# TensorE in order of emission through the attention and the retention, and 18 filling steps ahead of the first scores

## The chip, the core and the metric

The kernel runs on one core of a Trainium2 chip. A core has five engines with an instruction queue each: TensorE (PE, matrix products; its weight loads are shown as PEld), VectorE (DVE), ScalarE (ACT), GpSimd (POOL) and SyncE (SP, which here only starts DMAs). Each engine works through its queue in order; where an instruction needs a result of another engine, it waits, and all that stands behind it in the same queue waits with it. The metric is the device time of one execution in microseconds (us); less is better.

## The reference

One layer of an encoder trunk, for 1024 tokens of 1024 features in float32:

```python
h = _swiglu(_rms_norm(x, ffn1_pre_norm[l]), ffn1_w_in[l], ffn1_w_out[l])
x = x + 0.5 * _rms_norm(h, ffn1_post_norm[l])
m = _token_mixing(_rms_norm(x, mix_pre_norm[l]), w_mix_in[l], ret_decay_fwd[l], ret_decay_bwd[l],
                  na_rel_bias[l], w_ret_out[l], w_na_out[l], w_mix_out[l], pos)
x = x + _rms_norm(m, mix_post_norm[l])
h = _swiglu(_rms_norm(x, ffn2_pre_norm[l]), ffn2_w_in[l], ffn2_w_out[l])
x = x + 0.5 * _rms_norm(h, ffn2_post_norm[l])
```

The middle part, `_token_mixing`, projects the tokens once with a wide matrix, and uses the pieces for two kinds of mixing:

```python
y = _bidirectional_retention(q, k, heads(rv, RET_V_DIM), decay_fwd, decay_bwd)   # 4 heads, chunks of 128 tokens
y_ret = (jax.nn.silu(rg) * y) @ w_ret_out
y_na = _neighborhood_attention(na_heads(nq), na_heads(nk), na_heads(nv), rel_bias) @ w_na_out  # 8 heads of 64
merged = jax.nn.sigmoid(g_ret) * y_ret + jax.nn.sigmoid(g_na) * y_na
return merged @ w_out
```

The neighbourhood attention lays the tokens on a grid of 16 rows and 64 columns; each query sees a window of 8 rows and 16 columns, with a learned bias per head, and takes a softmax over it.

## The kernel before

Every product is made of three products of split operands (`mm3`, lines 85 to 89): a float32 tile x is split by ACT into a rounded high part (`split`, line 60) and by DVE into the rest (line 61), and TensorE adds high by high, low by high and high by low. So each operand that TensorE reads costs one ACT and one DVE instruction first.

The program runs through these stages: the first feed-forward block, the projections for the mixing, the neighbourhood attention, the retention, the output projections, the second feed-forward block. The change touches the attention and the retention.

**The attention** (`na_cores`, line 688) works on 32 units: 4 pairs of heads by 8 units of 128 queries each. It is written as a pipeline over units:

- `scores` of unit i: for each of the two heads of the pair, two matmuls of 128x384 (line 744: high and low part of the query), then on DVE the bias and the maximum (745) and the negated maximum (747), on ACT the exponential (749), on DVE the reciprocal of the sum and the scaling (751, 753).
- `flip` of unit i-1: six transposes on TensorE (763) into two PSUM banks `pt`, then the split into `pth` (ACT) and `ptl` (DVE).
- `values` of unit i-2: nine matmuls of 128x256 (`mm3` with `vh`, `vl`), then two ACT copies into `ot` (779).

Between these parts stand calls of a **filler**. `fill(n)` takes n steps from the generator `products()`; a step is one `mm3`, three matmuls of 128x512 of the value projection of the retention (operands `wh`, `wl` with `a11h` and the like, 128 steps), then of the gates (384 steps in all), which nothing in the attention waits for. `NA_FILL` gives the numbers: 12 steps ahead of the first scores, then 2 after `scores` and 2 after `values` in each of 34 iterations. Filling steps of the projections bring their own loads and splits of weights (`wraw`, `wh`, `wl`).

At a change of the pair of heads the keys (`kraw`), the queries (`qraw`) and, for each group of columns, the values (`vraw`) are loaded by SP and split by ACT, DVE and POOL; the bias tiles `bt` are loaded by SP for nearly every unit.

**The retention** (`ret_cores`, line 872) works through 4 heads of 8 chunks: a backward pass that builds states (`update`), then per chunk a score product, the state update, the two products with the states (`cross`), the product `inner`, a norm, and two transposes two chunks later (`store`, 966). Filling steps stand between these too (`RET_FILL`): 14 ahead of the first transposes of the keys (`kdec`, 914), 2 to 4 at each place after that, and 2 ahead of each of the last three `store`. What the filler still holds after that is drained.

**What sets the order.** The order in which the Python code emits instructions isn't the order in the queues. Emission gives priorities; a scheduler then simulates the program with durations of its own, and puts next on each engine the instruction of the highest priority that is ready in its simulation. So an instruction that the simulation shows as waiting is passed by later ones that are ready: filling steps, scores of later units, or values. The queues are fixed then; the chip keeps to them whatever the real durations are.

Of the kernel before, what the change touches and what calls it, by code (L numbers as in the profile page):

```python
# [1 line left out]

# [1 line left out]

# [22 lines left out]
RH = 4  # L27
NHP = 4

NA_FILL = (12, 2, 2)  # L30
RET_FILL = (14, 2, 2, 4, 2, 3, 0, 1, 2)
FLIP_FILL = (8, 8, 8, 8, 2)
NA_UNITS = ((0, 0, 0), (3, 1, 0), (1, 0, 1), (1, 0, 2), (4, 1, 1), (4, 1, 2), (2, 0, 3), (5, 1, 3))
# [4 lines left out]
class Core:  # L38
# [97 lines left out]
    def out_proj(self, nk, lhs, wload, done, groups=((0, 1, 2), (3, 4, 5), (6, 7)), tail=3, lag=8, space=3):  # L136

        left = []  # L140

        def one(t, k, a, w):
            for e in [e for e in left if e[0] <= 0]:
                left.remove(e)
                f = e[1]()
                if f is not None:
                    left.append([2, f])
            for b in range(2):
                self.mm3(banks[t][b], a[t], w[b], k == 0, k == nk - 1)
            for e in left:  # L150
                e[0] -= 1

        for toks in groups:
            banks = {t: [self.bank() for _ in range(2)] for t in toks}
            tl = tail if len(toks) > 1 else 0
            for k in range(nk - tl):
                w, a = wload(k), lhs(k, toks)
                for t in toks:
                    one(t, k, a, w)
            last = [(k, lhs(k, toks), wload(k)) for k in range(nk - tl, nk)]  # L160
            for t in toks:
                for k, a, w in last:
                    one(t, k, a, w)
                f = done(t, banks[t])
                if f is not None:
                    left.append([max(lag, max([e[0] for e in left], default=-space) + space), f])
        return [f for _, f in left]


class Filler:  # L170
# [267 lines left out]
class LeftFactors:  # L438


    order = [j + h * FT // 2 for j in range(FT // 2) for h in range(2)]
# [588 lines left out]
def trunk_layer(ctx: ExitStack, tc, x, g1a, w1i, w1o, g1b, gma, wmt, wnv, wrv, logits, dtab, rope, bias,  # L1030
# [7 lines left out]
    c = Core(tc, const, wpool, psum, dram)  # L1038
# [219 lines left out]

    fill = Filler(products())
    dec = []  # L1260
    with tc.tile_pool(name="na", bufs=1) as na:
        na_cores(c, na, d, bias, fill, *NA_FILL, {24: lambda: dec.append(Decays(c, mix, logits, dtab))})
    dec = dec[0]
    fill.until("rv")
    with tc.tile_pool(name="ret", bufs=1) as ret:
        ret_cores(c, ret, mix, d, dec, fill, RET_FILL)
    y_stack = ExitStack()
    ypool = pool(y_stack, "y")
# [152 lines left out]
```

## Time and profile before

| | |
|---|---|
| median of 3 runs | 2334.3 us (2330.53 to 2337.57) |
| profiled execution | 2332.5 us, its span 2330.7 us |
| first feed-forward block and projections | 0 to about 998 us |
| attention (first filling step to last values) | 998 to 1232 us |
| retention | about 1232 to 1471 us |
| output projections and second feed-forward block | 1471 to 2331 us |
| PE idle outside 1000 to 1480 us | some 70 us, at the start, the end, and the borders of the feed-forward blocks |

Times in the profile are counted from the start of the span. "Busy" is the time in which an engine works on an instruction; matmuls overlap, so the start of one to the start of the next is the price of a matmul, not its duration. PEclk is the clock granted to TensorE as a share of full speed.

### The profile page before, as it was taken

Reading aid. Unit: us, or ns where it says so; the run is one execution under the profiler, and the core shown is the slowest. Engines: PE = TensorE matmul, PEld = TensorE weight load, DVE = VectorE, ACT = ScalarE, POOL = GpSimd, SP = SyncE. Lnnn points to the kernel's source line nnn. Section 1 sums busy time; section 2 is a strip of 40 time slices with the busy share of each in tenths; the row PEclk is TensorE's granted clock in tenths of the full one; section 3 lists DMA queues with packets and bytes.
Section 4 is the critical chain, followed back from the end, with each engine's and each line's share of the span. In section 5 each row is a group of like instructions: output and inputs, shape, how many; then the busy total and the mean of one; then the engine's idle time right before and its main releaser. Section 6 shows DMA issues by size and latency. Waiting matters only on the chain.

```text
span 2330.7 us, 30323 instructions
## 1 busy us (share of the span) xinstructions
PE 2226.6 (96%) x10288; PEld 1849.4 (79%) x10288; DVE 1677.0 (72%) x2939; ACT 1008.0 (43%) x2104; POOL 598.9 (26%) x749
## 2 busy tenths in 40 slices
PE   6999999999998999989889999998889999999998
PEld 5888888778886888877768888887668888887886
DVE  7887777745878588867865678545887778775575
ACT  6332222344553223367765676324633222234453
POOL 3144343300440144311101222101322434431032
PEclk9999999999998999999989999999999999999999
DMA  5355555576753444466634467765524555547674
GB/s 190 109 181 174 197 177 185 199 233 189 257 175 112 168 131 131 137 217 202 195 107 152 161 222 231 263 230 188 194 91 142 197 176 200 181 154 235 190 243 142
DMA packets 161884, 422.64 MB, mean 181 GB/s; under 512 B 19712, under 2 KB 47488, under 8 KB 161664
## 3 DMA queue, kind: packets, MB, share of 16 engines
q1 hardware_dynamic: 121248, 286.97, 38.4%
q0 software_dynamic: 40480, 133.72, 15.6%
q8 instruction: 81, 1.33, 0.2%
q14 instruction: 75, 0.61, 0.1%
HBM read 301.60 MB, written 123.21 MB: 182 GB/s over the span
## 4 chain that ended last, share of the span: by engine, by line
PE 84%; issue 6%; DVE 4%; DMA 2%; ACT 2%; POOL 1%; SPq 0%; POOLq 0%; DVEq 0%; ACTq 0%
PE ps L87 26%; PE ps L88 26%; PE ps L89 26%; PE pt L88 1%; PE pt L89 1%; PE pt L87 1%; DMA graw<-g0a 1%; PE pt L126 1%; DVE tmp L117 0%; DVE wl L61 0%; DMA graw<-m 0%; PE pt L914 0%; DMA kraw<-nk 0%; PE pt L966 0%; DVE gl L61 0%
## 5 line engine op out<-in xcount | busy, mean ns | idle before, releaser
L61 DVE TENSOR_TENSOR wl<-wraw,wh 128x512 fp32r<-128x512 f32 x662 | 460.3, 719 | 97.4 <-ACT wh L60 94.5
L60 ACT CAST wh<-wraw 128x512 fp32r<-128x512 f32 x670 | 391.7, 619 | 277.3 <-PE ps L88 110.0
L87 PE MATMUL ps<-wh,gh 128*128 128x512 f32 x612 | 239.2, 393 | 17.2 <-ACT gh L60 12.8
L88 PE MATMUL ps<-wl,gh 128*128 128x512 f32 x612 | 239.4, 391 | 0.0
L61 DVE TENSOR_TENSOR gl<-graw,gh 128x512 fp32r<-128x512 f32 (+2 forms) x178 | 128.9, 728 | 149.2 <-ACT gh L60 146.0
L89 PE MATMUL ps<-wh,gl 128*128 128x512 f32 x612 | 229.1, 392 | 1.1 <-DVE gl L61 1.1
L60 ACT CAST gh<-graw 128x512 fp32r<-128x512 f32 (+2 forms) x178 | 106.5, 602 | 210.6 <-PE ps L88 72.0
L87 PEld LDWEIGHTS ps<-wh,gh 128*128 128x128 f32 x612 | 115.5, 189 | 44.8 <-ACT gh L60 12.9
L526 POOL TENSOR_TENSOR q<-q,gain 128x512 f32<-128x512 f32 x30 | 58.1, 1958 | 334.4 <-PE ps L88 122.1
L89 PEld LDWEIGHTS ps<-wh,gl 128*128 128x128 f32 x612 | 114.8, 188 | 26.3 <-DVE gl L61 2.8
L88 PEld LDWEIGHTS ps<-wl,gh 128*128 128x128 f32 x612 | 115.5, 189 | 23.7
L60 ACT CAST wh<-t 128x512 fp32r<-128x512 f32 x58 | 36.1, 623 | 192.7 <-DVE t L384 192.6
L87 PE MATMUL ps<-a11h,wh 128*128 128x512 f32 x280 | 113.1, 404 | 1.9 <-DVE tmp L226 1.9
L89 PE MATMUL ps<-a11h,wl 128*128 128x512 f32 x280 | 111.7, 399 | 0.0
L88 PE MATMUL ps<-a11l,wh 128*128 128x512 f32 x280 | 111.4, 398 | 0.0
L87 PE MATMUL ps<-a12h,wh 128*128 128x512 f32 x280 | 110.6, 395 | 0.1
L88 PE MATMUL ps<-a12l,wh 128*128 128x512 f32 x280 | 109.8, 392 | 0.0
L89 PE MATMUL ps<-a12h,wl 128*128 128x512 f32 x280 | 109.6, 391 | 0.0
L87 PE MATMUL ps<-a22h,wh 128*128 128x512 f32 x280 | 109.5, 391 | 0.0
L89 PE MATMUL ps<-a22h,wl 128*128 128x512 f32 x280 | 109.2, 390 | 0.0
L88 PE MATMUL ps<-a22l,wh 128*128 128x512 f32 x280 | 109.1, 389 | 0.0
L400 DVE TENSOR_TENSOR c<-ps,gt 128x512 f32<-128x512 f32 x44 | 30.4, 691 | 107.2 <-PE ps L89 107.1
(362 smaller groups left out, 6006.6 us busy)
## 6 DMA issues: line engine op xcount, KB each, us to landing
wraw<-in_dram SPq DMA_DIRECT2D x243, 512.0 KB, 4.3
lead<-in_dram POOLq DMA_DIRECT2D x44, 256.0 KB, 3.9
g0s<-cmb POOLq DMA_DIRECT2D x44, 256.0 KB, 3.2
graw<-g0s SPq DMA_DIRECT2D x44, 256.0 KB, 2.8
wq<-in_dram POOLq DMA_DIRECT2D x44, 256.0 KB, 3.8
g1s<-cmb POOLq DMA_DIRECT2D x44, 256.0 KB, 2.7
graw<-g1s SPq DMA_DIRECT2D x44, 256.0 KB, 2.7
bt<-in_dram SPq DMA_DIRECT2D x24, 384.0 KB, 3.9
```

Source lines behind the costliest of these rows:

```text
L60: nc.scalar.copy(h, src)
L61: (eng or nc.vector).tensor_tensor(l, src, hf, ALU.subtract)
L87: mm(ps, a[0], b[0], start=start, stop=False, skip_group_check=more)
L88: mm(ps, a[0], b[1], start=False, stop=False, skip_group_check=more)
L89: mm(ps, a[1], b[0], start=False, stop=stop, skip_group_check=more)
L126: self.nc.tensor.transpose(pt[:, j * P:(j + 1) * P], h[:, j * P:(j + 1) * P], self.ident)
L400: self.last = self.read = tt(c21, p7, c12, ALU.add).ins
L526: (eng or c.nc.gpsimd).tensor_tensor(h if out is None else out, h, self.post[:, b * 512:(b + 1) * 512], ALU.mult)
```

## The change

```diff
-from contextlib import ExitStack
+from contextlib import ExitStack, contextmanager
...
-NA_FILL = (12, 2, 2)
+NA_FILL = (18, 2, 2)
...
+@contextmanager
+def in_order(c, engine):
+
+    traced = c.nc.cur_bb.bb.instructions
+    n = len(traced)
+    yield
+    prev = None
+    for i in c.nc.cur_bb.bb.instructions[n:]:
+        if i.engine == engine:
+            if prev is not None:
+                c.tc.add_manual_dep(i, prev.name, mybir.DependencyInfo(
+                    mybir.DependencyClass.NoSync, mybir.DependencyReason.DATA), reason="order")
+            prev = i
...
-    with tc.tile_pool(name="na", bufs=1) as na:
+    with tc.tile_pool(name="na", bufs=1) as na, in_order(c, mybir.EngineType.PE):
         na_cores(c, na, d, bias, fill, *NA_FILL, {24: lambda: dec.append(Decays(c, mix, logits, dtab))})
     dec = dec[0]
     fill.until("rv")
-    with tc.tile_pool(name="ret", bufs=1) as ret:
+    with tc.tile_pool(name="ret", bufs=1) as ret, in_order(c, mybir.EngineType.PE):
         ret_cores(c, ret, mix, d, dec, fill, RET_FILL)
```

`in_order` gives each PE instruction that is emitted inside the block a dependency on the PE instruction emitted before it. The dependency is of a kind that adds no semaphore and no wait: it only tells the scheduler that the one comes after the other. So inside the attention, and again inside the retention, TensorE's queue stands in the order of the code, filling steps included. The first instruction of a block has no such tie, and the other engines have none; their queues come from the same simulation, which now runs with another TensorE. The second edit puts 18 filling steps ahead of the first scores in place of 12; the six steps are missing at the end, since the filler holds the same 384 steps (and a mark behind the value projection that a call counts as one). Before, all calls together ask for 384 of these 385; now they ask for 390, and the last ones come up empty.

On each engine the kernel has the same instructions as before, but for two ACT_TABLE_LOAD on ACT that fall away. All queues are the same up to the first scores. From there to the output projection of the mixing they differ; behind that they are the same again.

The first place is TensorE's queue from the end of the second unit's scores to the fourth's, with the first transposes (`s` into `pt`) and the first of the nine value matmuls (`pth`, `vh`); the numbers tell buffers apart. Before:

```order
L744 MATMUL ps_8742<-k1_8603,ql_8623 128x384
L744 MATMUL ps_8807<-k0_8602,qh_8704 128x384
L744 MATMUL ps_8807<-k0_8602,ql_8705 128x384
L744 MATMUL ps_8811<-k1_8603,qh_8708 128x384
L744 MATMUL ps_8811<-k1_8603,ql_8709 128x384
L763 MATMUL pt_8775<-ident_69,s_8687 128x128 x3
L763 MATMUL pt_8781<-ident_69,s_8687 128x128 x3
L87 MATMUL ps_8843<-pth_8773,vh_8768 128x256
L744 MATMUL ps_8863<-k0_8602,qh_8753 128x384
L744 MATMUL ps_8863<-k0_8602,ql_8754 128x384
L744 MATMUL ps_8867<-k1_8603,qh_8757 128x384
L744 MATMUL ps_8867<-k1_8603,ql_8758 128x384
```

In the changed kernel, from the second unit's scores to the same transposes (lines are 15 higher behind `in_order`, so scores are L759 and transposes L778):

```order
L759 MATMUL ps_8766<-k0_8602,qh_8618 128x384
L759 MATMUL ps_8766<-k0_8602,ql_8619 128x384
L759 MATMUL ps_8770<-k1_8603,qh_8622 128x384
L759 MATMUL ps_8770<-k1_8603,ql_8623 128x384
L87 MATMUL ps_8627<-wh_8746,a12h_5400 128x512
L88 MATMUL ps_8627<-wl_8747,a12h_5400 128x512
L89 MATMUL ps_8627<-wh_8746,a12l_5401 128x512
L87 MATMUL ps_8628<-wh_8746,a12h_5400 128x512
L88 MATMUL ps_8628<-wl_8747,a12h_5400 128x512
L89 MATMUL ps_8628<-wh_8746,a12l_5401 128x512
L778 MATMUL pt_8803<-ident_69,s_8715 128x128 x3
L778 MATMUL pt_8809<-ident_69,s_8715 128x128 x3
```

Before, the scores of three units stand ahead of the first transposes, and no filling step between them and the transposes; now there are the scores of two, with two filling steps behind the second. The count of filling matmuls ahead of these transposes is 72 in both.

The second place is TensorE's queue four units later. Before:

```order
L744 MATMUL ps_9102<-k0_8602,qh_8975 128x384
L744 MATMUL ps_9102<-k0_8602,ql_8976 128x384
L744 MATMUL ps_9106<-k1_8603,qh_8979 128x384
L744 MATMUL ps_9106<-k1_8603,ql_8980 128x384
L87 MATMUL ps_9147<-pth_9066,vh_8907 128x256
L744 MATMUL ps_9169<-k0_8602,qh_8975 128x384
L744 MATMUL ps_9169<-k0_8602,ql_8976 128x384
L744 MATMUL ps_9173<-k1_8603,qh_8979 128x384
L744 MATMUL ps_9173<-k1_8603,ql_8980 128x384
L763 MATMUL pt_9135<-ident_69,s_9037 128x128 x3
L88 MATMUL ps_9147<-ptl_9067,vh_8907 128x256
L89 MATMUL ps_9147<-pth_9066,vl_8908 128x256
```

In the changed kernel, at about the same unit, from the last value matmul to the next filling step:

```order
L89 MATMUL ps_9175<-pth_9094,vl_8936 128x256
L87 MATMUL ps_8826<-wh_9147,a22h_6071 128x512
L88 MATMUL ps_8826<-wl_9148,a22h_6071 128x512
L89 MATMUL ps_8826<-wh_9147,a22l_6072 128x512
L87 MATMUL ps_8824<-wh_9151,a12h_5400 128x512
L88 MATMUL ps_8824<-wl_9152,a12h_5400 128x512
L89 MATMUL ps_8824<-wh_9151,a12l_5401 128x512
L759 MATMUL ps_9197<-k0_8602,qh_9003 128x384
L759 MATMUL ps_9197<-k0_8602,ql_9004 128x384
L759 MATMUL ps_9201<-k1_8603,qh_9007 128x384
L759 MATMUL ps_9201<-k1_8603,ql_9008 128x384
L87 MATMUL ps_8825<-wh_9151,a22h_6071 128x512
```

Before, the value matmuls of one unit are taken apart, and scores, transposes and values follow each other with no filling step between; the steps stand in long rows elsewhere. Now every unit has its six transposes and nine value matmuls together, and two filling steps stand on each side of the scores.

At the end of the retention the last `store` calls lose steps: after the last product with a state there stood some seven filling steps, two of them between the last two pairs of transposes; now two stand there, and the last two pairs follow each other.

## The prediction

> **What bounds the kernel.** I read the page's first part, then the stages by a table of windows, then TensorE's waits in the stages that the change touches.
>
> ```profile
> PE 2226.6 (96%) x10288; PEld 1849.4 (79%) x10288; DVE 1677.0 (72%) x2939; ACT 1008.0 (43%) x2104; POOL 598.9 (26%) x749
> core 0: us, PE busy (x) PEld busy (x) DVE busy (x) ACT busy (x) POOL busy (x), PEclk, DMA share, GB/s
> 1007.00:1232.00 225.00, 196.14 (x1042) 167.51 (x1041) 159.59 (x467) 155.26 (x393) 19.73 (x26) 0.93 0.55 172
> 1246.00:1472.00 226.00, 224.61 (x1290) 195.82 (x1289) 164.67 (x428) 140.90 (x365) 54.57 (x86) 1.00 0.59 191
> ```
>
> TensorE is the bound of the whole (96% busy), so the change can gain only where TensorE stands still or runs slowly. The attention (1007 to 1232) is such a place: 28.9 us idle, at a mean clock of 0.93. The retention (1246 to 1472) isn't: 1.4 us idle at full clock. The waits of the attention by who ended them:
>
> ```profile
> PE ps L87 <- ACT pth L60: 15.5, 11, 3.6
> PE pt L763 <- DVE s L753: 4.8, 2, 4.4
> PE ps L88 <- DVE ptl L61: 4.8, 4, 2.5
> PE ps L744 <- DVE nast L745: 2.0, 2, 1.0
> PE pt L763 <- DVE ptl L61: 1.6, 3, 0.7
> ```
>
> They add up to 28.7 us, 20.3 of them value matmuls that wait for their transposed weights (`pth`, `ptl`). The clock costs as well. One such wait, and the stretches in which the clock was half (the first of six, and the sum):
>
> ```profile
> 1202.63 0.54 PE L87 MATMUL ps<-pth,vh 128*128 128x256 f32 x1 [2.81 <-ACT pth L60]
> 1202.97 0.52 PE L744 MATMUL ps<-k,qh 128*128 128x384 f32 x1
> 1203.29 0.52 PE L744 MATMUL ps<-k,ql 128*128 128x384 f32 x1
> ...
> 1021.80:1028.60 6.80, 4.52 (x14) 3.76 (x15) 5.80 (x19) 5.57 (x16) 0.54 (x1) 0.50 0.88 337
> ...
> sum 30.60, PE 25.98 PEld 21.69 DVE 21.53 ACT 17.72 POOL 0.54; mean PE 4.33 PEld 3.62 DVE 3.59 ACT 2.95 POOL 0.09
> ```
>
> After the 2.81 us wait a score matmul takes 0.32 us from start to start (1202.97 to 1203.29). TensorE was busy for 25.98 us at half clock, so 13.0 us would do at full clock. Waits and clock together: 28.7 + 13.0 = 41.7 us that the attention could lose at most by this count.
>
> **The attention, part by part.** No work is added; what counts is how it is spread. The prices at full clock, from start to start:
>
> ```profile
> 1044.80 0.82 PE L763 MATMUL pt<-ident,s 128*128 128x128 f32 x6
> 1045.37 0.36 PE L87 MATMUL ps<-pth,vh 128*128 128x256 f32 x1
> ...
> 1046.52 0.34 PE L744 MATMUL ps<-k,qh 128*128 128x384 f32 x1
> ...
> 1047.24 0.40 PE L89 MATMUL ps<-wh,a12l 128*128 128x512 f32 x1
> 1047.48 0.40 PE L87 MATMUL ps<-wh,a22h 128*128 128x512 f32 x1
> ```
>
> Six transposes cost 0.57, nine value matmuls 1.15, four score matmuls 0.72, and a filling matmul 0.23 to 0.24, so a step of three 0.69. An iteration of the new order has these and four steps: 0.57 + 1.15 + 0.72 + 2.76 = 5.2 us. Between the transposes of a unit and its values now lie the values of the unit before, four steps and the next scores and transposes: 1.15 + 2.76 + 0.72 + 0.57 = 5.2 us, where the quoted order of before had as little as nothing but scores. That is what takes the waits for `pth` and `ptl` away.
>
> What stays is the start:
>
> ```profile
> 1015.47 2.30 ACT L60 CAST k<-kraw 64x512 fp32r<-64x512 f32 x4 [0.62 <-DMA kraw<-nk]
> 1019.70 1.28 ACT L749 ACT_TABLE_LOAD   x1
> 1021.00 0.61 ACT L749 ACTIVATE s<-s,nast 128x384 f32<-128x384 f32 x1
> 1023.01 1.66 PE L763 MATMUL pt<-ident,s 128*128 128x128 f32 x6 [4.40 <-DVE s L753]
> ```
>
> The first transposes wait for the first exponentials, and those stand on ACT behind the next pair's keys and a table load; ACT's queue is the same there in the changed kernel. As many filling matmuls (72) stand ahead of these transposes as before, and ahead of the first score matmul 54 in place of 56, since the scheduler had moved them forward on its own. So 18 steps in place of 12 buy nothing by themselves: they keep what the tie would take, six steps (4.1 us) of cover while the first queries come in. I keep the start's two waits (1.0 and 4.4) and half of its 4.52 us at half clock: 41.7 - 5.4 - 2.3 = 34.0 us go.
>
> A second count goes by the pieces from the first transposes, at 1023.0, to the last value matmul:
>
> ```profile
> 1232.19 0.28 PE L89 MATMUL ps<-pth,vl 128*128 128x256 f32 x1
> ```
>
> That is 209.3 us, in which before does some six steps more and four score matmuls fewer than the new order will: 206 us. The new order's pieces are 32 x 0.57 + 32 x 1.15 + 30 x 0.72 + 127 x 0.69 = 164 us, and 2.3 for the start's clock: 39 us less. I take 36, between the two.
>
> Then the other engines become the question, since the work of DVE in this stretch has to fit into less time:
>
> ```profile
> 1022.90:1232.50 209.60, 186.06 (x997) 159.81 (x998) 148.05 (x441) 143.99 (x370) 15.71 (x22) 0.93 0.52 161
> 1160.00:1177.00 17.00, 17.00 (x98) 15.04 (x98) 14.27 (x52) 12.84 (x35) 0.00 (x0) 1.00 0.58 177
> 1065.00:1114.00 49.00, 48.30 (x273) 41.94 (x273) 38.38 (x104) 36.38 (x93) 3.69 (x5) 0.99 0.64 189
> ```
>
> In 209.6 - 36 = 174 us DVE's 148.05 us are 85%, ACT's 143.99 are 83%. In two stretches of this same stage TensorE ran without a stop at a DVE share of 84% (14.27 of 17.00) and almost so at 78% (38.38 of 49.00). At 84% the stretch takes 176 us, 2 more; at 78% it takes 189, 15 more. I take **6 us** given back, nearer to the first row; bounds 0 and 15. Of waits that remain, two may again be followed by a stretch of 3.4 us at half clock, 1.7 us each: **3.4 us** given back; bounds 0 and the 13.0 of before.
>
> [...] The wait of 2.81 us above was followed by half clock. [...]
>
> **The retention.** At its start two waits stand before, and what the second queue would do:
>
> ```profile
> PE pt L914 <- issue: 1.8, 1, 1.8
> PE pt L914 <- DVE kdl L64: 1.5, 1, 1.5
> ...
> 1236.90 4.11 DMA kraw<-rk
> ...
> 1243.60 1.13 ACT L60 CAST qh<-qraw 128x512 fp32r<-128x512 f32 x2
> 1244.63 1.02 ACT L60 CAST vh<-vraw 128x256 fp32r<-128x256 f32 x3
> ```
>
> The keys land at 1241.0, 8.8 us after the last values. Now 48 filling matmuls (11 us) lie between, so the first wait goes; and two steps stand between the two groups of transposes. But the splits of `qraw` and `vraw` (1.13 and 1.02) now stand ahead of `kdh` in ACT's queue, and the first state update may wait for it for about a microsecond. 3.3 - 1.0 = **2.3 us** gained; bounds 0 and 5 (with the clock). Inside the retention TensorE has no wait to lose. A chunk's four steps and its own products (some 4.7 us) lie between each result and its use, so I cost the tie at 0; the cover gone, it would cost the wait itself, at most the 3 us of the next chain once per head.
>
> At its end the six steps are missing:
>
> ```profile
> 1465.51 0.48 ACT L949 ACTIVATE y<-ps,decq 128x256 f32<-128x256 f32 x1 [1.29 <-PE ps L89]
> 1467.92 0.51 ACT L957 ACTIVATE yn<-y,rstd 128x256 f32<-128x256 f32 x1 [0.94 <-POOL rstd L97]
> 1470.10 0.38 PE L966 MATMUL pt<-ident,yn 128*128 128x128 f32 x2
> 1471.67 0.50 PE L87 MATMUL ps<-xy,wh 128*128 128x512 f32 x1 [1.19 <-ACT xy L60]
> ```
>
> From the last state product to `yn` the norm takes about 3 us (1465.5 to 1468.4). Twenty filling matmuls covered it; six (1.4 us) do now. **1.5 us** lost; bounds 0 and 3. The 1.19 us wait stays.
>
> **Sum**: 36 - 6 - 3.4 + 2.3 - 1.5 = 27.4 us off the profiled execution's own 2332.5 us: 2305 us. The median of before, 2334.3, lies 1.8 above that execution, well inside the spread of its three runs.
>
> **Rivals.**
>
> *DVE and ACT set the pace.* At the 78% row 15 us come back, with the clock of half the old stretches (6.5) on top: 36 - 15 - 6.5 + 1 = 15, **2317 us**. For it: ACT too would be 83% busy. Against it: the 84% row.
>
> *The waits only change place* (loads of queries, biases and keys now have to land in 43 us a pair of heads instead of 52): **2332 us**. For it: ACT waited 12.8 us for `qraw` before. Against it: at a DMA share of 0.64 TensorE was at 99%. That the tie does nothing is excluded by the quoted order.
>
> *Slower: a strict order passes every hold on.* A unit's transposes come after its scores by three pairs of steps, transposes, values and scores: 4.1 + 0.57 + 1.15 + 0.72 = 6.6 us. The chain in between:
>
> ```profile
> L745 DVE CUSTOM_DVE_ANT_0 s<-ps,bt 128x384 f32<-128x384 f32 x64 | 33.6, 553 | 12.7 <-PE pt L763 12.7
> L753 DVE TENSOR_SCALAR s<-s,ss 128x384 f32<-128x384 f32 x64 | 23.9, 417 | 0.7
> L749 ACT ACTIVATE s<-s,nast 128x384 f32<-128x384 f32 x64 | 38.9, 610 | 8.5 <-DVE nast L747 8.4
> L63 ACT ACTIVATE qh<-qraw 128x256 fp32r<-128x256 f32 x32 | 12.7, 414 | 13.2 <-DMA qraw<-nq 12.8 <-PE ps L744 0.2
> ```
>
> Two of each of the first three are 3.2 us; I allow 0.5 for the small instructions between, so 2.9 us are spare. A hold on ACT or DVE beyond that stops TensorE, and no later scores may pass. It loses from the point where the mean hold in 32 units is above 2.9 + 36/32 = 4.0 us; at 4.5 it costs 32 x 1.6 = 51 against 36: **2347 us**. Against it: the last row's holds are 12.8 us in all.
>
> [...]
>
> **How the numbers follow.** Forecast 0.63, DVE and ACT's pace 0.17, waits that change place 0.08, slower 0.08, the rule 0.04. About 0.3% (7 us) is what a measurement can tell from no change. Faster holds the first, second and last case: 0.84; the third and fourth are 0.08 each. The best bounds, 39 + 5, give 2288; the worst of the first two cases, 34 - 15 - 6.5 - 1.5, give 2322 (11 us off). That leaves out the last 2 in 10.
>
> **What would show it.** Right: in 1007 to about 1195 waits for `pth` and `ptl` of a few microseconds in all, a clock above 0.97, DVE at 83 to 88%, and the first transposes still waiting some 4 to 5 us. Wrong: waits of transposes for the scaled scores (`s`) in every unit, or a DVE without a pause beside an idle TensorE; waits for `sfl`, `al` or `yn` inside the retention.

## The result and the profile after

The changed kernel takes **2309.24 us** (median of 4 runs, 2309.06 to 2312.12) against 2334.52 us before (median of 4 runs, 2330.53 to 2337.57): ratio 0.9893, 95% interval 0.9876 to 0.9909. The profiled execution took 2309.06 us (span 2307.2; before 2330.7). 25 us went, where 29 were forecast for the medians (2334.3 to 2305) and 27.4 for the profiled executions.

TensorE's line of the page, then the attention and the inside of the retention in a table of windows of the changed kernel (columns as in the prediction; the attention now ends 23 us earlier, at 1209):

```profile
PE 2216.3 (96%) x10288; PEld 1842.7 (80%) x10288; DVE 1677.2 (73%) x2939; ACT 1003.8 (44%) x2102; POOL 597.9 (26%) x749
```

```profile
1007.00:1209.00 202.00, 183.64 (x1027) 158.18 (x1026) 158.31 (x466) 150.19 (x389) 20.05 (x26) 0.97 0.61 192
1223.00:1446.00 223.00, 222.77 (x1287) 194.54 (x1285) 165.51 (x422) 138.43 (x362) 51.73 (x82) 1.00 0.58 192
```

The attention's idle time fell from 28.9 to 18.4 us and its mean clock rose from 0.93 to 0.97; the retention has nothing to lose, as before. What TensorE waits for in the attention of the changed kernel (line, what released it: us in total, times, longest us; lines are 15 higher than before):

```profile
PE pt L778 <- DVE s L768: 13.8, 6, 4.0
PE ps L759 <- ACT qh L63: 1.7, 1, 1.7
PE pt L778 <- DVE ptl L61: 1.5, 2, 0.8
PE ps L759 <- ACT ev L1154: 0.7, 1, 0.7
PE pt L778 <- DVE dect L850: 0.5, 1, 0.5
```

The 20.3 us in which values waited for `pth` and `ptl` are gone to the last one. In their place transposes wait for the scaled scores `s`: 13.8 us, six times, where it was 4.8. The sum is 18.2 us in place of 28.7. The large ones of them and the end of the retention, in TensorE's timeline of the changed kernel (start, duration, instruction, in brackets the idle time ahead and its releaser):

```profile
1022.56 1.66 PE L778 MATMUL pt<-ident,s 128*128 128x128 f32 x6 [3.38 <-DVE s L768]
...
1065.58 1.01 PE L778 MATMUL pt<-ident,s 128*128 128x128 f32 x6 [3.67 <-DVE s L768]
...
1114.70 1.57 PE L778 MATMUL pt<-ident,s 128*128 128x128 f32 x6 [4.00 <-DVE s L768]
...
1448.34 0.44 PE L981 MATMUL pt<-ident,yn 128*128 128x128 f32 x2 [2.57 <-ACT yn L972]
1449.95 1.65 PE L87 MATMUL ps<-xy,wh 128*128 128x512 f32 x3 [1.18 <-ACT xy L60]
```

The first is the start. The second is the change to the second pair of heads, the third the change to the third pair. The last two are the end of the retention. Each of the three waits of the attention is followed by a stretch at half clock (windows of the changed kernel; the last number but two of a row is the clock):

```profile
1022.80:1026.20 3.40, 3.40 (x12) 2.83 (x12) 1.39 (x4) 3.40 (x10) 1.45 (x3) 0.50 0.98 318
1067.10:1070.50 3.40, 3.40 (x12) 2.82 (x11) 1.66 (x4) 0.64 (x3) 0.00 (x0) 0.51 0.66 219
1114.90:1118.30 3.40, 3.40 (x16) 3.37 (x16) 1.85 (x5) 1.71 (x6) 0.00 (x0) 0.50 0.43 150
```

That is 10.2 us at half clock, so 5.1 lost, where six stretches had cost 13.0.

To compare all kernels, I added up for each trace, stage by stage, TensorE's idle time and half of its busy time at half clock. "Start" goes from 1003 us to 2 us behind the beginning of the first transposes, "attention" from there to the last value matmul, "ret. start" is the next 25 us, "ret. end" goes from 12 us ahead of the last transposes of `yn` to 8 behind, "behind" from there to 2290, "ahead" is from the first matmul, at about 8.5 us, to 1003. An idle time that crosses a border counts where it begins. The inside of the retention is left out (at most 1.3 us in each).

```
us lost            ahead  start  attention  ret.start  ret.end  behind
before              28.3    7.3       34.6        5.0      1.2    33.7
changed             28.6    6.0       17.4        0.0      5.1    31.3
attention tied      25.5    6.0       17.5        0.0      6.3    30.0
retention tied      28.0    7.9       39.4        8.6      1.2    33.9
both tied, 12       26.9    7.6       21.9        1.7      1.2    32.6
untied, 18          26.4    0.5       23.3        0.7      7.6    31.5
untied, 24          28.3    0.0       29.6        2.9      6.6    32.1
tied, 24            27.3    3.3       25.4        0.6      9.1    31.2
tied, fill 3/1      28.5    4.8       12.0        0.2      6.5    30.8
tied, fill 1/3      27.5    5.8       25.2        0.0      6.5    31.8
tied, fill 4/0      27.1    4.3       14.6        2.1      5.4    29.7
end steps           28.5    6.0       15.7        0.0      1.2    31.4
keys on DVE         26.0    6.9       14.6        0.0      5.5    34.2
3/1 and end steps   28.0    5.3       15.1        0.3      1.5    29.2
```

From before to changed: 1.3 at the start, 17.2 in the attention, 5.0 at the retention's start, -3.9 at its end, 2.4 behind, -0.3 ahead: 21.7 of the 23.5 us by which the span is shorter. "Ahead", where no kernel differs, runs from 25.5 to 28.6 from one execution to the next, so a difference of 2 or 3 us in a cell of "ahead" or "behind" says nothing. One of 3 us, or even 5, in the attention says little by itself either: "changed", "attention tied" and "end steps" have the same queues there and lost 17.4, 17.5 and 15.7 us, "fill 3/1" and "3/1 and end steps" 12.0 and 15.1, "before" and "retention tied" 34.6 and 39.4.

### The profile page after: what moved, and what is told of

It reads as the page before. It is cut to its first block, busy times and chain, and to the rows that moved or that the text cites. A ratio compares the mean times of both kernels' runs of the same rounds, so it can differ in the third digit from the quotient of the medians.

```text
span 2307.2 us, 30283 instructions
## 1 busy us (share of the span) xinstructions
PE 2216.3 (96%) x10288; PEld 1842.7 (80%) x10288; DVE 1677.2 (73%) x2939; ACT 1003.8 (44%) x2102; POOL 597.9 (26%) x749
## 4 chain that ended last, share of the span: by engine, by line
PE 87%; DVE 6%; DMA 3%; ACT 2%; issue 1%; POOL 1%; SPq 0%; DVEq 0%; POOLq 0%; ACTq 0%
PE ps L87 27%; PE ps L88 27%; PE ps L89 27%; PE pt L88 1%; PE pt L89 1%; PE pt L87 1%; DVE wl L61 1%; PE pt L778 1%; PE ps L759 1%; DMA graw<-g0a 1%; DMA graw<-m 1%; DVE x L551 1%; PE pt L126 0%; DMA wraw<-in_dram 0%; DVE tmp L117 0%
## 5 line engine op out<-in xcount | busy, mean ns | idle before, releaser
L87 PE MATMUL ps<-wh,gh 128*128 128x512 f32 x612 | 240.3, 394 | 15.1 <-ACT gh L60 10.7
```

The costliest lines, as they stand in the source:

```text
L87: mm(ps, a[0], b[0], start=start, stop=False, skip_group_check=more)
```

## The experiments

All are edits of the changed kernel. Of the two tied blocks and the count 12 or 18, four combinations beside before and changed were run, then what sets the remaining waits.

**The attention tied alone.**

```diff
-    with tc.tile_pool(name="ret", bufs=1) as ret, in_order(c, mybir.EngineType.PE):
+    with tc.tile_pool(name="ret", bufs=1) as ret:
```

> The attention tied (18 steps ahead), the retention left to the scheduler. Theory A (the gain is the even spread of filling steps in the attention; the retention has no waits to win): 2306 to 2312 us, within 3 us of the changed kernel, with the attention as in the changed kernel and the wait of about 2.6 us for yn at the end of the retention kept. Theory B (the tie in the retention brings a part of its own, above all at its start): 2315 us or more.

2308.49 us (2306.67 to 2310.23), ratio 0.9892 (0.9879 to 0.9906), the same as the whole change. The tie of the retention is worth nothing that can be measured.

**The retention tied alone**, with 12 steps.

```diff
-    with tc.tile_pool(name="na", bufs=1) as na, in_order(c, mybir.EngineType.PE):
+    with tc.tile_pool(name="na", bufs=1) as na:
...
-NA_FILL = (18, 2, 2)
+NA_FILL = (12, 2, 2)
```

> The retention tied, the attention left to the scheduler, 12 steps ahead. Theory A: no gain, and a loss at the start of the retention: the scheduler takes the filling steps of the retention's first 14 into the attention, 11 filling matmuls (2.5 us) are left between the last values and the first transposes of the keys, which land some 9 us after those values, so a wait of 6 to 7 us there in place of 3.3; 2334 to 2341 us. Theory B: 2327 us or less.

2336.56 us (2330.66 to 2340.68), ratio 1.0009 (1.0000 to 1.0018): no gain, as expected. The forecast wait at the retention's start is there, in TensorE's timeline of this kernel:

```profile
1245.72 1.09 PE L929 MATMUL pt<-ident,kraw 128*128 128x128 f32 x4 [6.34 <-issue]
```

**Both tied, 12 steps.**

```diff
-NA_FILL = (18, 2, 2)
+NA_FILL = (12, 2, 2)
```

> Both stages tied, with 12 filling steps ahead of the first scores. Theory A (the steps ahead only cover the first queries): TensorE reaches the first scores 4.1 us earlier and waits about 4 us for the queries, but five steps come back at the end of the retention and take its wait of 2.6 us and a stretch at half clock away; in sum within 3 us of the changed kernel, 2306 to 2312 us. Theory B (the 18 steps carry a good part of the gain): 2316 us or more.

2314.39 us (2309.2 to 2317.08), ratio 0.9915 (0.9901 to 0.9928): a miss, 5 us above the changed kernel, though the intervals just overlap. Its waits of the attention, and the longest of them:

```profile
PE pt L778 <- DVE s L768: 16.4, 6, 5.2
PE ps L759 <- issue: 3.6, 1, 3.6
PE ps L759 <- ACT qh L63: 1.6, 1, 1.6
```

```profile
1028.52 1.57 PE L778 MATMUL pt<-ident,s 128*128 128x128 f32 x6 [5.24 <-DVE s L768]
```

The first scores now wait for 3.6 us, which 18 steps cover. The first transposes wait for nothing; it is the second unit's that wait 5.24 us (in the changed kernel the first wait 3.38 and the second 0.65). From the first scores to the second unit's transposes that makes 10.4 us against 5.8: 4.6 more, about the 4.1 us of cover that the prediction put on the six steps under the tie. In return the end of the retention keeps its steps and has no wait for `yn`.

**18 steps, nothing tied.** Both `in_order` taken out as above.

> No tie, 18 filling steps ahead. Theory A: no gain, since the scheduler still packs scores and values without filling steps between; more steps ahead of the first transposes may take 3 to 4 us at the start, the missing steps cost 3 us at the end of the retention; 2329 to 2337 us. Theory B (the 18 steps carry a good part of the gain): 2325 us or less.

2315.32 us (2312.84 to 2316.64), ratio 0.992 (0.9907 to 0.9934). The theory fell: six steps more, without any tie, bring 19 of the 25 us. Its largest waits of the attention:

```profile
PE ps L87 <- ACT pth L60: 10.9, 10, 2.1
PE pt L778 <- DVE ptl L61: 2.7, 5, 0.9
PE ps L88 <- DVE ptl L61: 2.5, 3, 1.9
```

They are of the kind of before (values that wait for `pth` and `ptl`), only shorter. At the start 42 filling matmuls stand in the queue between the first score matmul and the first transposes, where before had 16 and the tied kernels with 2 and 2 have 18, and the start's loss goes from 7.3 to 0.5 us: 6.8 of the gain. 11.3 us come from the attention (7.1 of them clock: short waits are followed by half clock less often, see the last section) and 4.3 from the retention's start, and 6.4 are lost again at its end.

**24 steps, nothing tied**, to tell whether that gain belongs to the steps or to the order that came out. Both `in_order` are out here too.

```diff
-NA_FILL = (18, 2, 2)
+NA_FILL = (24, 2, 2)
```

> Neither the attention nor the retention tied, 24 filling steps ahead of the first scores. With 18 and no tie the time was 2315.3, with 12 and no tie (the kernel before) 2334. Theory A (the steps ahead give TensorE something to do while the first queries and exponentials come, and with 18 that start is covered already): 24 changes little, 2312 to 2319 us, no wait above 1 us at the start, the end of the retention with a wait for yn of 3.4 us or more. Theory B (the count only made the scheduler's simulation come out with another order, a lucky one): another count gives another order, with waits of over 22 us between 1007 and 1210 us, and 2322 us or more.

2321.07 us (2318.88 to 2322.55), ratio 0.9953 (0.9941 to 0.9964): between the two ranges, and neither theory holds whole. The waits of the attention add up to 19.7 us, not to over 22, and the wait for `yn` is 2.54 us, not 3.4 or more. The start stays covered (0.0 us lost, with 33 filling matmuls between the first score matmul and the first transposes), so the 7 us there came with both counts. The attention loses 29.6 us in place of 23.3, with waits such as this one, 6 transposes and then the first value matmul:

```profile
1137.27 0.82 PE L778 MATMUL pt<-ident,s 128*128 128x128 f32 x6
1142.36 0.58 PE L87 MATMUL ps<-pth,vh 128*128 128x256 f32 x1 [4.27 <-ACT pth L60]
```

So the rest of the untied gain hangs on which order the scheduler's simulation gives for a count. Why it is better for 18 than for 12 or 24 is left open.

**24 steps, both tied.** The same edit of the count, with the ties.

> The changed kernel with 24 filling steps ahead of the first scores. From 12 to 18 under the tie brought 5 us; with 18 the first scores still wait 1.75 and the first transposes 3.37 us, followed by 3.4 us at half clock. Theory A (the steps cover the start): these waits fall from 5.1 to about 1 us and the half clock goes (1.7), six more steps are missing at the end of the retention (1.4 to 2.5 us): 2303 to 2307 us. Theory B (ACT's and DVE's work of the start moves back with the scores, so the waits stay): 2309 to 2313 us.

2318.41 us (2316.41 to 2321.98), ratio 0.9944 (0.9931 to 0.9957): both theories missed, it is 9 us slower than with 18. TensorE's timeline of this kernel at the start, and at the end of the retention:

```profile
1018.44 0.50 PE L87 MATMUL ps<-wh,a21h 128*128 128x512 f32 x1 [2.59 <-ACT ev L1154]
1018.77 0.40 PE L88 MATMUL ps<-wl,a21h 128*128 128x512 f32 x1
1019.01 0.39 PE L89 MATMUL ps<-wh,a21l 128*128 128x512 f32 x1
...
1023.61 1.09 PE L778 MATMUL pt<-ident,s 128*128 128x128 f32 x6 [0.74 <-DVE s L768]
...
1456.64 1.20 PE L981 MATMUL pt<-ident,yn 128*128 128x128 f32 x4 [4.55 <-ACT yn L972]
```

The first transposes hardly wait any more (0.74). But a filling step itself now waits 2.59 us: its accumulator must have been copied out (`ev`, on ACT), and in the tied queue nothing may pass it. At the end the wait for `yn` grows to 4.55. These two explain 1 us net (start 2.7 better, end 4.0 worse); the other 8 are in the attention (25.4 against 17.4, 5 of it clock), whose queue is the same but for the phase of the filler. There transposes wait 2.40 us at 1030.6 and 2.11 at 1165.2, and a filling step 2.77 at 1116.4, which the changed kernel has not; their cause wasn't traced.

**The two fillings of an iteration, 3 and 1.** Three steps between scores and transposes, one behind the values.

```diff
-NA_FILL = (18, 2, 2)
+NA_FILL = (18, 3, 1)
```

> The changed kernel with 3 filling steps after the scores and 1 after the values, in place of 2 and 2: the same steps, but a unit's transposes come seven steps after its scores, not six (0.69 us more), and the way from transposes to values is as long as before. Theory C (what is left of the waits is the chain from scores to transposes that overruns the distance in a strict order): each of the waits of transposes (4.0, 3.7, 3.4, 1.4 and five under 1 us) gets 0.7 us shorter, 4 to 6 us in all; 2303 to 2306 us. Theory D (DVE's or ACT's total work sets the pace): no change, 2307 to 2311 us.

2304.72 us (2302.69 to 2307.07), ratio 0.9878 (0.9863 to 0.9893). Within what theory C gave, though its interval overlaps that of 2 and 2; the waits for `s` halve:

```profile
PE pt L778 <- DVE s L768: 7.3, 4, 3.1
PE pt L778 <- DVE ptl L61: 2.0, 1, 2.0
```

**1 and 3.** The same line with `(18, 1, 3)`.

> The changed kernel with 1 step after the scores and 3 after the values: the distance from scores to transposes is five steps, 0.69 us less. Theory C: the nine waits of transposes get 0.7 us longer, and units that had less than that to spare begin to wait; 7 to 20 us more, 2316 to 2329 us. Theory D: no change, 2307 to 2311 us.

2316.13 us (2313.26 to 2317.92), ratio 0.9924 (0.9912 to 0.9937), at the near end of what the distance theory gave; DVE's and ACT's pace alone would not have changed with the place of a step. Its waits:

```profile
PE pt L778 <- DVE s L768: 18.6, 10, 4.3
```

**4 and 0.** The same line with `(18, 4, 0)`.

> The changed kernel with 4 steps after the scores and none after the values: the distance is eight steps, 1.38 us more. Theory C: the waits under 1.4 us go and the three long ones lose 1.4 each, some 8 us, with less of the half clock behind them; 2298 to 2303 us. Theory D: no change, 2307 to 2311 us.

2305.83 us (2301.46 to 2307.12), ratio 0.9877 (0.9864 to 0.9891): no further gain, a miss. The waits for `s` fall again, but what they lose others win:

```profile
PE pt L778 <- DVE ptl L61: 4.8, 3, 2.2
PE pt L778 <- DVE s L768: 4.2, 3, 2.4
```

**Steps kept for the end.** Three instead of four steps in one place of each head of the retention.

```diff
-RET_FILL = (14, 2, 2, 4, 2, 3, 0, 1, 2)
+RET_FILL = (14, 2, 2, 3, 2, 3, 0, 1, 2)
```

> The changed kernel with 3 steps in place of 4 at the place in each retention head behind the forward kdec, which leaves four steps more for the last transposes of the retention. Theory A: the wait for yn (2.6 us) and the stretch at half clock behind it (1.7 us) go, 3 to 4 us; 2305 to 2307 us. Rival: the wait moves into the heads, where the first state update now comes a step earlier; 2308 to 2312 us.

2303.85 us (2299.53 to 2305.59), ratio 0.9869 (0.9856 to 0.9883), a little below theory A's range. The last transposes of this kernel wait for nothing, and only the old 1.18 us stays:

```profile
1443.56 0.38 PE L981 MATMUL pt<-ident,yn 128*128 128x128 f32 x2
1445.12 1.19 PE L87 MATMUL ps<-xy,wh 128*128 128x512 f32 x4 [1.18 <-ACT xy L60]
```

**The keys' second half on DVE.** What holds the exponentials at a change of heads? First ACT's timeline of the changed kernel there, then DVE's, then POOL's:

```profile
1058.05 1.14 ACT L60 CAST k<-kraw 64x512 fp32r<-64x512 f32 x2
1059.21 1.08 ACT L1154 COPY ev<-ps 128x512 f32<-128x512 f32 x2
...
1061.58 0.63 ACT L764 ACTIVATE s<-s,nast 128x384 f32<-128x384 f32 x1
```

```profile
1057.65 0.16 DVE L762 TENSOR_SCALAR nast<-nast 128x2 f32<-128x2 f32 x1
1057.84 1.78 DVE L61 TENSOR_TENSOR k<-kraw,k 64x512 fp32r<-64x512 f32 x1
1059.65 1.40 DVE L64 SCALAR_TENSOR_TENSOR ql<-qraw,qh 128x256 fp32r<-128x256 f32 x1
1061.08 0.69 DVE L61 TENSOR_TENSOR k<-kraw,k 64x512 fp32r<-64x512 f32 x1
```

```profile
1057.79 1.29 POOL L61 TENSOR_TENSOR k<-kraw,k 64x512 fp32r<-64x512 f32 x1 [0.59 <-DVE ql L64]
1059.26 1.50 POOL L61 TENSOR_TENSOR k<-kraw,k 64x512 fp32r<-64x512 f32 x1 [0.19 <-ACT k L60]
```

The exponential's bias (`nast`) is ready at 1057.8 and it starts at 1061.58, behind casts of queries and keys, copies of accumulators (`ev`) and two more splits on ACT; DVE's own work beside POOL's is slow (1.78 us for one instruction on the keys, 0.69 after POOL's have ended). The edit takes POOL out:

```diff
-                c.split(kop[hp][e][es, bs], kop[hp][e][es_, bs], kr[es, bs], eng=nc.gpsimd if hp and b else None)
+                c.split(kop[hp][e][es, bs], kop[hp][e][es_, bs], kr[es, bs], eng=None)
```

> The changed kernel, but the low parts of the second half of each key block are computed on DVE, not on POOL. In the changed kernel DVE's instruction on the keys takes 1.78 us and one on the queries 1.40 us beside POOL's, and 0.69 and 0.42 us without it; the transposes at the two changes of a pair of heads wait 3.67 and 4.0 us. Theory A (ACT is the hold there: its casts of keys and queries stand ahead of the exponentials, and DVE's delay lies beside them): the two waits stay within 0.5 us of what they were, 2307 to 2311 us. Theory B (DVE's slow instructions are the hold): each wait falls below 3 us and the time is 2303 to 2306.5 us.

2309.5 us (2308.19 to 2312.17), ratio 0.9905 (0.9892 to 0.9917): no gain. The wait at the first change of heads falls from 3.67 to 2.86 us and the second from 4.0 to 3.26, but that at the start grows from 3.38 to 4.86, which wasn't traced (with the changed kernel's queues it was 2.04 to 3.61 in three traces). The first, in TensorE's timeline, and the keys on DVE in DVE's:

```profile
1062.31 1.04 PE L778 MATMUL pt<-ident,s 128*128 128x128 f32 x4 [2.86 <-DVE s L768]
```

```profile
1055.42 1.29 DVE L61 TENSOR_TENSOR k<-kraw,k 64x512 fp32r<-64x512 f32 x2
1056.74 0.43 DVE L64 SCALAR_TENSOR_TENSOR ql<-qraw,qh 128x256 fp32r<-128x256 f32 x1
1057.20 1.29 DVE L61 TENSOR_TENSOR k<-kraw,k 64x512 fp32r<-64x512 f32 x2
```

By its time theory A holds, by its waits (within 0.5 us of what they were) it doesn't; the 1.5 us saved at the two changes are about what the start lost in this trace. What holds the two, the traces show. The next windows (columns as in the prediction) go, for the unit whose transposes wait, from its first maximum on DVE to its scaling, the last step ahead of the transposes: at the first and the second change of heads in the changed kernel, then the same two in this one:

```profile
1055.76:1065.03 9.27, 5.43 (x31) 4.27 (x29) 9.14 (x22) 9.15 (x22) 4.37 (x5) 1.00 0.80 251
1104.98:1114.14 9.16, 5.72 (x34) 4.72 (x32) 9.04 (x21) 6.65 (x16) 3.15 (x2) 1.00 0.47 144
```

```profile
1053.33:1061.75 8.42, 5.64 (x32) 4.44 (x30) 8.29 (x24) 8.29 (x21) 1.62 (x3) 1.00 0.79 236
1102.14:1110.55 8.41, 5.71 (x34) 4.71 (x32) 8.28 (x23) 6.57 (x16) 0.00 (x0) 1.00 0.52 156
```

DVE works almost without a pause in all four (9.14 of 9.27 us, 9.04 of 9.16), on its queue of keys, queries, weights, transposed weights, values and the next unit's maxima. With that queue, an exponential that came earlier could have brought the scaling forward by no more than the 0.13 us in which DVE stood idle; at the second change ACT itself stood idle for 2.5 us. The edit spared DVE 0.86 and 0.75 us on keys and queries, the stretches got 0.85 and 0.75 us shorter, and the waits 0.81 and 0.74. So DVE's queue is the hold at both changes. Theory B was nearer, but the slowness beside POOL is a small part of that queue. Whether another order of DVE's queue, with the scaling ahead of later units' work, would take the waits away, no run tested.

**3 and 1 together with the steps for the end.** The edits of those two runs in one kernel.

> The changed kernel with two changes of its counts together: three filling steps between scores and transposes and one behind the values (alone 2304.7 us), and three instead of four steps in one place of each retention chunk, which leaves steps for the end (alone 2303.9 us). Theory A (they act in different stages and add up: 4.5 and 5.4 us off 2309.2): 2297.5 to 2301 us, and no wait for yn. Theory B (they share a gain, such as the half clock behind 1440 us or the order of the out-projection): 2302 to 2305 us.

**2298.07 us** (2294.78 to 2301.97), ratio 0.9855 (0.9839 to 0.9871): they add up (0.0015 and 0.0024 below the changed kernel's ratio, 0.0038 together). This beats both kernels, and its interval lies clear of the changed kernel's; each of the two alone overlaps it.

## Why the prediction was right

The time came out 4 us above the forecast, well inside the range, and the main mechanism was right. But the start and the attention together gave 18.5 us where 36 - 6 - 3.4 = 26.6 were forecast; the retention's start gave 2.7 us more than forecast, and its end took 2.4 more. That the sum is no further off is in part luck: 2.4 us behind and 1.8 us outside the table's cells came from no term, and are no more than one execution differs from the next.

- **The tie removes the waits for `pth` and `ptl`**: right, 20.3 us to none, and the attention tied alone gives the whole gain.
- **The start keeps its loss** (7.7 us of the attention's 41.7 kept): right, 6.0 measured (before 7.3 by the table's count). The transposes of the start still wait 3.38 us and half clock follows. The tied order has 18 filling matmuls between the first scores and the first transposes with 12, 18 and 24 steps ahead, as the reason said. What the number of steps ahead changes is where the waits fall: with 12 at the first scores and the second unit's transposes, with 24 at a filling step.
- **Six us given back to DVE's share, 3.4 to the clock**: the first was mis-sized. Behind the start the table has 17.4 us lost where 9.4 were forecast: about 13.2 of waits, 4.2 of clock (two stretches, as forecast, and the rest of the start's). The price came from DVE's mean share (84% in a stretch without waits). The larger part of the waits doesn't come from the mean but from two moments, 7.7 us at the changes of a pair of heads, where the next pair's keys and queries and other units' work stand in DVE's queue between a unit's maximum and its scaling. The prediction took 3.2 + 0.5 us for that chain; there it lasts 9.3 and 9.2 us, almost all of it DVE's. That is one of the prediction's own signs of being wrong, "a DVE without a pause beside an idle TensorE", at two places, and the mechanism of the rival "a strict order passes every hold on", at a size below its point of decision: six waits in 32 units, not one in each. That it is the distance from scores to transposes that counts is shown by 1/3, 2/2 and 3/1: 18.6, 13.8 and 7.3 us of waits for `s` (9.2 in the kernel with 3/1 and the end steps), and by their times.
- **18 steps buy nothing by themselves**: wrong. Under the tie they keep the cover, as said (from 12 to 18 brings 5 us). But without the tie they give 19 us alone. The step failed because it counted the matmuls ahead of the first transposes under the tie and took them for those of an untied queue, where the scheduler puts 42 in place of 16 between the first scores and the first transposes. The two parts of the change are substitutes in part: 20 us for the tie alone, 19 for the steps alone, 25 together.
- **The retention's start, 2.3 us gained**: 5.0, at its upper bound. The tie of the attention does it: with the retention untied the table has 0.0 us there as well, and 48 or 49 filling matmuls stand ahead of the first transposes in both. No wait for `kdh` took the place, and the half clock went with the wait.
- **The inside of the retention, 0**: right, by the run with the attention tied alone.
- **Its end, 1.5 us lost**: 3.9 by the table; the wait was 2.57 us and 3.4 us at half clock came with it. The term had left out the clock. That it was the missing steps is shown by the run that keeps them: no wait, ratio 0.9869.
- **The second feed-forward block**: not in the sum, 2.4 us better in the trace, no more than it differs between executions.

The rivals: "waits only change place" fell with the gain, "the tie does nothing" with the order. "DVE and ACT set the pace" fell as a mean: DVE was busy for 158.31 of 202 us (78%; up to 1200 us it was 80%, where 83 to 88% had been named as a sign of being right), and with the same work 3/1 is 4.5 us faster and 1/3 7 us slower. At the two changes of heads it holds, for DVE. The last case, with its chance of 0.04, was that the short waits that remain bring no half clock. It fell with the clock rows: in the changed kernel half clock (0.50 from 1449.4 to 1452.8) followed the wait of 2.57 us at the retention's end, and in the kernel with 3/1 one of 1.85 us:

```profile
1012.85 0.44 PE L759 MATMUL ps<-k,qh 128*128 128x384 f32 x1 [1.85 <-ACT qh L63]
```

```profile
1010.74:1014.15 3.41, 1.54 (x6) 0.94 (x6) 2.05 (x5) 1.87 (x5) 0.00 (x0) 1.00 1.05 337
1014.15:1017.56 3.41, 3.41 (x10) 2.66 (x9) 3.11 (x9) 2.35 (x5) 0.53 (x1) 0.50 1.02 419
```

## What to carry to other kernels

Here a queue that follows the code turned many waits between neighbours into a few at the places where another engine's work comes in a lump; after tying an order, look there first, and try more independent work between producer and consumer rather than evenly around them (3 and 1 was better than 2 and 2, 4 and 0 no better than that). Filling work is finite and has results of its own to be taken away: more of it at the start is missing at the end (2.57 and 4.55 us waits for `yn`), and a step can wait itself (2.59 us with 24 tied steps). A count that a scheduler turns into an order moves the whole order, so its effect can't be read from the place where the count stands.

## What the hardware showed that was not expected

**DVE beside POOL.** In the changed kernel DVE's key instruction took 1.78 us while POOL ran the same operation and 0.69 us after POOL's had ended, and the one on the queries 1.40 us (rows above) in place of 0.42 at 1057.31, ahead of POOL's; the two slow ones end 0.54 and 0.29 us after POOL's do. Giving half of the keys to POOL saved DVE nothing there, it cost 0.86 us: its two key instructions took 1.78 + 0.69 = 2.47 us and the late query 1.40, where four take 2 x 1.29 = 2.58 and the query 0.43.

**Half clock after short waits, but not after each.** It followed a wait of 1.85 us in one kernel, and didn't follow the wait of 2.59 us quoted from the kernel with 24 tied steps (its next matmuls start 0.24 us apart). In each of the 14 kernels' traces, all stretches at half clock begin on one grid of 3.413 us, to within 3 ns, and but for one at the very end of a trace they are that long or a multiple. The two waits lie differently in the windows of that grid. The 1.85 us lay in one (1010.74 to 1014.15, above); the 2.59 us were cut by a border, at 1016.66, into 0.81 and 1.78:

```profile
1013.25:1016.66 3.41, 2.60 (x13) 1.93 (x11) 1.69 (x3) 2.29 (x5) 0.47 (x1) 1.00 1.03 392
1016.66:1020.07 3.41, 1.63 (x7) 1.38 (x8) 3.26 (x5) 3.37 (x8) 3.33 (x4) 1.00 0.64 221
```

Over all windows at full clock behind the first 30 us of the 14 traces, half clock followed none of 8893 with less than 1.5 us idle and all 120 with more than 1.9; between the two it followed 23 of 59 (in the traces of before and changed alone: none of 1273, all 19, 4 of 10). A window at half clock was followed by another when at least 0.8 us of it were idle (all 85), and by full clock when less than 0.3 us were (all 127). So in these traces a wait of 2 to 3 us cost itself, and by where the grid cut it 1.7 us more or nothing.
